# A hybrid attention block: the scores of a unit's two heads computed together, in three 64-row passes

## The chip, the cores and the metric

The kernel runs on one core of a Trainium2 chip. The metric is device time of one execution in microseconds, the median over several executions; lower is better. The times of the kernel before are 1458.97, 1459.27 and 1465.46 us, so its median is 1459.27 us.

## The reference, cut to what matters

One layer: a normalised input is projected, two kinds of attention run on it, and an output projection and a squared-ReLU MLP follow. The part that the change touches is the attention. There are 8 stick-breaking heads and 4 differential heads with two maps each, over 1024 positions; every head or map has 64 columns of q and of k:

```python
# stick-breaking, for each of 8 heads
z = jnp.einsum('bhqd,bhkd->bhqk', qb, kh) * scale          # d = 64
w = where(causal, exp(log_sigmoid(z) + reverse_cumsum(log_sigmoid(-z))), 0)
out = jnp.einsum('bhqk,bhkd->bhqd', w, vh)
# differential, for each of 4 heads, with two maps
s1 = einsum(q1, k1) * scale + bias;  s2 = einsum(q2, k2) * scale + bias   # d = 64
a = softmax(s1) - lam * softmax(s2)
out = jnp.einsum('bhqk,bhkd->bhqd', a, vh)
```

## The kernel before, in words

All matrix products are made from float32r parts: an operand is split into a high part and the rest (the low part), and a product is the sum of high x high, high x low and low x high.

The attention is worked in eight **units** (the loop at L511): units 0 to 3 hold two stick-breaking heads each (`steps_sb`, L312), units 4 to 7 hold one differential head with its two maps (`steps_diff`, L370). So a unit always has two score matrices, here called its two heads. Rows 0 to 63 of a projected q or k belong to the first, rows 64 to 127 to the second.

The score of one head uses all 128 rows of TensorE. `project_q` (L204) writes one tile `qs` for each head, with the high part of its q on its own 64 rows and the low part stacked on the other 64. `project_k` (L218) writes for each head a tile `kh` and a tile `kl`, whose own 64 rows are copied by four DMAs to the other 64 (L230, L231): the doubled k. `scores` (L259) then needs two passes for one head and one chunk of at most 512 keys: `qs` x `kh` (L262) and `qs` x `kl` (L263). Each chunk takes one bank of PSUM under the tag `sc`, of which there are two.

A head's queries are taken in blocks `qt` of 128, two blocks to a step `j`, steps in the order 3, 1, 2, 0; block `qt` has `(qt+1)*128` keys, so a block of more than 512 keys has two chunks. In a stick-breaking unit the first head's four steps come first, then the second's. ScalarE turns each chunk into `rest` and `beta` (two sigmoids, L322 and L323), GpSimd masks the diagonal (L326), VectorE scans and multiplies (L331, L332). In a differential unit VectorE adds the bias and finds the minimum (L389), ScalarE takes the exponential (L394). One step later `finish_sb` (L296) or `finish_diff` (L339) transposes the weights on TensorE (L281), splits them (L287, L288) and multiplies them by v into a bank with the tag `av` (two banks); `finish_diff` also takes a second `av` bank for a sum of squares.

Between the steps the generator `fill` (L480) gives TensorE other work: the projections of the next unit and the gate projections (L196 to L198). Each step has a weight, and `total` (L518) says how the filler is spread over them. The tile framework places all instructions on each engine's queue ahead of time; a queue runs in the order in which it was written. After the units come the mixing of the branches (L567), the output projection (L656), and the MLP (L778, L954).

Of the kernel before, what the change touches and what calls it, by code (L numbers as in the profile page):

```python
# [12 lines left out]
ALU = mybir.AluOpType  # L13
# [28 lines left out]
def hybrid_block_kernel(  # L42
# [24 lines left out]
    ps = ctx.enter_context(tc.tile_pool(name="ps", bufs=1, space=PSUM))  # L67
# [9 lines left out]
    def any_tile(name, tags=("acc", "sc", "av")):  # L77
        turn[0] += 1
        return ps.tile([P, HALF], F32, tag=tags[turn[0] % len(tags)], name=name, bufs=2)
# [70 lines left out]
    with ExitStack() as actx:  # L150
# [4 lines left out]
        def normalised(c):  # L155

            xs = []
            for t in range(4 * c, 4 * c + 4):
                if t == 6:
                    last = pa.tile([P, 2, D], F32, tag="v", name="x_67", bufs=3)  # L160
                if t < 6:
                    xt = pa.tile([P, D], F32, tag="big_s" if t < 4 else "kh", name=f"x_{t}", bufs=4)
# [40 lines left out]

        def project_q(blk, name, scale, qs):  # L204

            qs += [pa.tile([P, S], F32R, tag="qs", name=f"qs_{name}_{a}", bufs=4) for a in range(2)]

            def done(c, cs, acc):
                for a, (own, other) in enumerate(((LO, HI), (HI, LO))):
                    nc.scalar.activation(qs[a][own, cs], acc[own], AF.Copy, scale=scale)  # L210
# [7 lines left out]
        def project_k(blk, name, kh, kl):  # L218

            kh += [pa.tile([P, S], F32R, tag="kh", name=f"kh_{name}_{a}", bufs=4) for a in range(2)]  # L220
            kl += [pa.tile([P, S], F32R, tag="kl", name=f"kl_{name}_{a}", bufs=4) for a in range(2)]

            def done(c, cs, acc):
                for a, own in enumerate((LO, HI)):
                    nc.scalar.copy(kh[a][own, cs], acc[own])
                    nc.vector.tensor_tensor(kl[a][own, cs], acc[own], f32(kh[a][own, cs]), op=ALU.subtract)

            yield from project(blk, name, done)
            for a, (own, other) in enumerate(((LO, HI), (HI, LO))):
                nc.sync.dma_start(out=f32(kh[a][other]), in_=f32(kh[a][own]))  # L230
                nc.sync.dma_start(out=f32(kl[a][other]), in_=f32(kl[a][own]))  # L231

        def project_v(grp, name, diff, vs):

            parts = early.pop(name, None) or [load_split(w_v[2 * grp + i], f"{name}_{i}") for i in range(2)]
            vs += [pa.tile([P, NT, 2 * P], F32R, tag="v", name=f"v_{name}_{u}", bufs=3) for u in range(2)]
# [22 lines left out]
        def scores(qs, kh, kl, qt, c0, c1, name):  # L259
            z = ps.tile([P, HALF], F32, tag="sc", name=name, bufs=2)  # L260
            q = qs[:, qt * P:(qt + 1) * P]
            nc.tensor.matmul(z[:, :c1 - c0], q, kh[:, c0:c1], start=True, stop=False)  # L262
            nc.tensor.matmul(z[:, :c1 - c0], q, kl[:, c0:c1], start=False, stop=True)  # L263
            return z[:, :c1 - c0]

        def score_tile(qt, name):
            if qt < 4:
                return pa.tile([P, HALF], F32, tag="small_s", name=name, bufs=4)
            return pa.tile([P, S], F32, tag="big_s", name=name, bufs=4)

# [24 lines left out]

        def finish_sb(u, a, j, w, v):  # L296
            av = ps.tile([P, HALF], F32, tag="av", name=f"av_{u}_{a}_{j}", bufs=2)
            for kb, qc, hi, lo in transposed(w, j, f"sb{u}_{a}_{j}"):
# [3 lines left out]
            part = pa.tile([P, 256], F32, tag="part", name=f"part_{u}_{a}_{j}", bufs=4)[LO]  # L302
            nc.scalar.copy(part, av[HI, 0:256])
            nc.vector.tensor_tensor(part, av[LO, 0:256], part, op=ALU.add)
            yt = pa.tile([P, 2, 256], F32R, tag="yt", name=f"yt_{u}_{a}_{j}")
            nc.scalar.copy(yt[LO, 0, :], part)
            nc.vector.tensor_tensor(yt[LO, 1, :], part, f32(yt[LO, 0, :]), op=ALU.subtract)
            nc.sync.dma_start(
                out=y_dram[u][a * DH:(a + 1) * DH, :, j * 256:(j + 1) * 256], in_=f32(yt[LO])
            )  # L310

        def steps_sb(u, qs, kh, kl, v):  # L312
            for a in range(2):
                for j in ORDER:
                    w = []
                    for qt in (2 * j, 2 * j + 1):
                        nk = (qt + 1) * P
                        name = f"{u}_{a}_{qt}"
                        beta, rest = score_tile(qt, f"beta_{name}"), score_tile(qt, f"rest_{name}")
                        for c0, c1 in chunks(nk):  # L320
                            z = scores(qs[a], kh[a], kl[a], qt, c0, c1, f"z_{name}_{c0}")
                            nc.scalar.activation(rest[:, c0:c1], z, AF.Sigmoid, scale=-1.0)  # L322
                            last_sigmoid[0] = nc.scalar.activation(beta[:, c0:c1], z, AF.Sigmoid)  # L323
                        dg = slice(nk - P, nk)
                        for tl, fill in ((rest, 1.0), (beta, 0.0)):
# [4 lines left out]
                        back = rest[:, nk - 1::-1]  # L330
                        nc.vector.tensor_tensor_scan(back, back, back, 1.0, op0=ALU.mult, op1=ALU.bypass)  # L331
                        nc.vector.tensor_tensor(  # L332
                            beta[:, :nk - 1], beta[:, :nk - 1], rest[:, 1:nk], op=ALU.mult
                        )
                        w.append(beta)
                    yield 4 * j + 3, partial(finish_sb, u, a, j, w, v)


        def finish_diff(h, j, w, v):  # L339
            av = ps.tile([P, HALF], F32, tag="av", name=f"avd_{h}_{j}", bufs=2)[:, 0:256]  # L340
            for kb, qc, hi, lo in transposed(w, j, f"df{h}_{j}"):
# [3 lines left out]
            yt, sq, r, w = (  # L345
                pa.tile([P, 256], F32, tag="part", name=f"{n}_{h}_{j}", bufs=4) for n in ("y", "sq", "r", "w")
            )
            nc.scalar.copy(yt, av)

            nc.scalar.activation(sq, yt, AF.Square)  # L350
            both = pa.tile([P, 2, 256], F32R, tag="yt", name=f"sqp_{h}_{j}")
            nc.scalar.copy(both[:, 0, :], sq)
            nc.vector.tensor_tensor(both[:, 1, :], sq, f32(both[:, 0, :]), op=ALU.subtract)
            ss = ps.tile([P, HALF], F32, tag="av", name=f"ss_{h}_{j}", bufs=2)[:, 0:256]
# [10 lines left out]
            both = pa.tile([P, 2, 256], F32R, tag="yt", name=f"yp_{h}_{j}")  # L365
# [4 lines left out]
        def steps_diff(h, qs, kh, kl, v):  # L370
# [5 lines left out]
            for j in ORDER:  # L376
                w = []
                for qt in (2 * j, 2 * j + 1):
                    nk = (qt + 1) * P
                    probs = []  # L380
                    sums = pa.tile([P, 2], F32, tag="sums", name=f"sums_{h}_{qt}", bufs=4)
                    for m in range(2):
                        name = f"{h}_{m}_{qt}"
                        s = score_tile(qt, f"s_{name}")
                        low = None
                        for c0, c1 in chunks(nk):
                            z = scores(qs[m], kh[m], kl[m], qt, c0, c1, f"z_{name}_{c0}")
                            prev, low = low, pa.tile([P, 1], F32, tag="low", name=f"low_{name}_{c0}", bufs=6)
                            nc.vector.tensor_tensor_reduce(  # L389
                                out=s[:, c0:c1], in0=z, in1=bias[:, S - nk + c0:S - nk + c1],  # L390
                                scale=1.0, scalar=BIG if prev is None else prev,
                                op0=ALU.add, op1=ALU.min, accum_out=low,
                            )
                        e = nc.scalar.activation(  # L394
                            s[:, :nk], s[:, :nk], AF.Exp, bias=low, scale=-1.0,
                            accum_out=sums[:, m:m + 1],
                        )
                        after_sigmoids(e)
                        probs.append(s)
# [8 lines left out]
                yield 4 * j + 3, partial(finish_diff, h, j, w, v)  # L408
# [15 lines left out]
        def setup_bias():  # L424
# [3 lines left out]
            for c in range(3):  # L428
# [5 lines left out]
                bvec = pa.tile([N_DIFF, 384], F32, tag="yt", name=f"bvec_{c}")  # L434
# [28 lines left out]
        def prepare(u):  # L463
# [5 lines left out]
            qs, kh, kl = [], [], []  # L469
            yield from project_q(qblk + h, f"{name}q{h}", scale, qs)  # L470
            yield from project_k(kblk + h, f"{name}k{h}", kh, kl)
# [4 lines left out]
            operands[u] = (qs, kh, kl, vs[u])  # L476
# [15 lines left out]
        qs, kh, kl, pair = [], [], [], []  # L492
        parts = [project_q(SBQ, "sbq0", SCALE, qs), project_k(SBK, "sbk0", kh, kl), project_v(0, "sbv0", False, pair)]
        early["sbv0"] = [
            load_split(
                w_v[i], f"sbv0_{i}", *(pa.tile([P, S], F32R, tag=n, name=f"{n}_sbv0_{i}", bufs=4) for n in ("qs", "kl"))
            ) for i in range(2)
# [588 lines left out]
```

## Time and profile before

| what | value |
|---|---|
| median of the runs (lowest, highest) | 1459.27 us (1458.97, 1465.46) |
| span of the profiled execution | 1456.6 us |
| TensorE (PE) busy | 1435.0 us, 99% of the span |
| VectorE (DVE) busy | 1016.5 us |
| ScalarE (ACT) busy | 742.3 us |
| GpSimd (POOL) busy | 321.2 us |

The profile gives the span of its execution, 1456.6 us; the median of the timed runs is 2.7 us above that. PE is busy when a matmul is under way, and PEld is the loading of its stationary operand (its weights), which overlaps the matmul ahead of it. A matmul's listed duration has a tail in which the next one already streams, so what a matmul costs PE is the time from its start to the next one's start. In the rows, `out<-in` names what is written and read by the program's names; the last figures before `x` are partitions by elements.

### The profile page before, as it was taken

How to read it: one execution, taken by the hardware profiler on the slowest of the kernel's cores; microseconds unless marked ns; L12 is line 12 of the kernel's file. 1: busy time of each engine (PE TensorE's matmuls, PEld its weight loads, DVE VectorE, ACT ScalarE, POOL GpSimd, SP SyncE). 2: the span in 40 equal slices, each digit the busy share in tenths (PEclk: the TensorE clock that was granted, in tenths of full speed). 3: DMA queues.
4: the chain of work that ended last, by engine and by line, in shares of the span. 5: the costliest groups of instructions: out<-in, count | busy, mean ns of one | idle time of the engine just before them, and what ended most of it. 6: DMA issues, size and time to landing. Idle time of an engine off the chain costs nothing.

```text
span 1456.6 us, 20071 instructions
## 1 busy us (share of the span) xinstructions
PE 1435.0 (99%) x7302; PEld 1220.3 (84%) x7302; DVE 1016.5 (70%) x1468; ACT 742.3 (51%) x1352; POOL 321.2 (22%) x312
## 2 busy tenths in 40 slices
PE   7999999999999999999999999999999999999997
PEld 6888898899889888888888878888888888888886
DVE  5477988898779876635556499767665669754783
ACT  6355765676556554763335364444444443534350
POOL 2022322231000000000002335333330357232611
PEclk9999999999999999999999999999999999999999
DMA  5241212221322245553437745544446785677681
GB/s 206 73 138 64 72 48 81 65 73 48 83 85 66 75 122 180 162 196 139 162 120 244 238 151 195 187 151 142 143 161 205 252 286 178 209 243 273 197 287 58
DMA packets 93946, 220.50 MB, mean 151 GB/s; under 512 B 9260, under 2 KB 24856, under 8 KB 93848
## 3 DMA queue, kind: packets, MB, share of 16 engines
q1 hardware_dynamic: 79448, 199.30, 42.8%
q10 hardware_dynamic: 14400, 19.93, 3.8%
q8 instruction: 57, 0.93, 0.3%
q14 instruction: 41, 0.34, 0.1%
HBM read 153.11 MB, written 60.05 MB: 146 GB/s over the span
## 4 chain that ended last, share of the span: by engine, by line
PE 94%; DVE 2%; DMA 1%; issue 1%; ACT 1%; POOL 0%; SPq 0%; POOLq 0%; DVEq 0%; ACTq 0%
PE dS L954 12%; PE dA L954 9%; PE mix L567 6%; PE o L656 6%; PE p_tr L778 5%; PE p_av L778 5%; PE c L778 4%; PE acc_gate L198 4%; PE acc_gate L196 4%; PE acc_gate L197 4%; PE p_sc L778 3%; PE z L263 2%; PE z L262 2%; PE tr_sb L281 2%; PE p L778 1%
## 5 line engine op out<-in xcount | busy, mean ns | idle before, releaser
L331 DVE TENSOR_TENSOR_SCAN rest<-rest 128x896 f32<-128x896 f32 (+3 forms) x64 | 87.6, 1374 | 20.6 <-POOL rest L326 20.3
L198 PE MATMUL acc_gate<-h_hi,lo_gate 128*128 128x512 f32 x256 | 101.0, 394 | 0.0
L196 PE MATMUL acc_gate<-h_hi,hi_gate 128*128 128x512 f32 x256 | 100.8, 394 | 0.0
L197 PE MATMUL acc_gate<-h_lo,hi_gate 128*128 128x512 f32 x256 | 100.7, 394 | 0.0
L608 DVE TENSOR_TENSOR lS_lo<-raw_S,lS_hi 128x1024 fp32r<-128x1024 f32 x32 | 56.2, 1757 | 39.8 <-ACT lS_hi L607 39.8
L326 POOL TENSOR_SCALAR_AFFINE_SELECT rest<-rest 128x128 f32<-128x128 f32 x64 | 23.5, 367 | 240.7 <-ACT rest L322 232.1
L954 PE MATMUL dS<-rT_hi,lS_hi 128*128 128x512 f32 x192 | 74.7, 389 | 0.0
L954 PE MATMUL dS<-rT_lo,lS_hi 128*128 128x512 f32 x192 | 74.7, 389 | 0.0
L954 PE MATMUL dS<-rT_hi,lS_lo 128*128 128x512 f32 x192 | 74.7, 389 | 0.0
L607 ACT CAST lS_hi<-raw_S 128x1024 fp32r<-128x1024 f32 x32 | 33.7, 1052 | 74.1 <-DMA raw_S<-s_dramS 33.8
L567 PE MATMUL mix<-y,hi_mix 128*128 128x512 f32 x256 | 68.6, 389 | 0.0
L394 ACT ACTIVATE s<-s,low 128x896 f32<-128x896 f32 (+7 forms) x64 | 49.7, 777 | 29.9 <-DVE low L389 29.7
L389 DVE CUSTOM_DVE_ANT_0 s<-z,bias 128x512 f32<-128x512 f32 (+3 forms) x64 | 37.0, 587 | 32.4 <-PE z L263 26.4
L567 PEld LDWEIGHTS mix<-y,hi_mix 128*128 128x128 f32 x256 | 48.0, 188 | 10.0
L198 PEld LDWEIGHTS acc_gate<-h_hi,lo_gate 128*128 128x128 f32 x256 | 48.2, 188 | 9.2
L197 PEld LDWEIGHTS acc_gate<-h_lo,hi_gate 128*128 128x128 f32 x256 | 48.2, 188 | 8.8
L196 PEld LDWEIGHTS acc_gate<-h_hi,hi_gate 128*128 128x128 f32 x256 | 48.2, 188 | 8.6
L116 POOL TENSOR_SCALAR rstd_o<-s 128x1 f32<-128x1 f32 x8 | 2.8, 356 | 236.5 <-DVE wa_lo L608 212.2
L287 ACT CAST wth_sb<-tr_sb 128x512 fp32r<-128x512 f32 (+1 forms) x80 | 41.2, 548 | 26.6 <-PE tr_sb L281 25.2
L326 POOL TENSOR_SCALAR_AFFINE_SELECT beta<-beta 128x128 f32<-128x128 f32 x64 | 53.9, 842 | 3.4 <-ACT beta L323 2.4
L288 DVE TENSOR_TENSOR wtl_sb<-tr_sb,wth_sb 128x512 fp32r<-128x512 f32 (+1 forms) x80 | 48.5, 627 | 7.7 <-ACT wth_sb L287 7.5
L778 PE MATMUL c<-hB_hi,wa_hi 128*128 128x512 f32 x128 | 50.0, 392 | 2.1 <-ACT p L798 2.1
(351 smaller groups left out, 4751.2 us busy)
## 6 DMA issues: line engine op xcount, KB each, us to landing
s_dramS<-us SPq DMA_DIRECT2D x64, 256.0 KB, 3.9
raw_S<-s_dramS SPq DMA_DIRECT2D x32, 512.0 KB, 4.4
s_dramA<-u ACTq DMA_DIRECT2D x48, 256.0 KB, 3.5
raw_A<-s_dramA SPq DMA_DIRECT2D x24, 512.0 KB, 3.8
raw_gate<-in_w_in_dram SPq DMA_DIRECT2D x16, 512.0 KB, 3.7
gate_dram<-gt SPq DMA_DIRECT2D x32, 256.0 KB, 2.5
y<-y_dram SPq DMA_DIRECT2D x16, 512.0 KB, 6.4
g<-gate_dram SPq DMA_DIRECT2D x16, 512.0 KB, 4.3
```

The costliest lines, as they stand in the source:

```text
L196: nc.tensor.matmul(acc, w_hi[:, ks], h_hi[k][:, cs], start=(k == 0), stop=False)
L197: nc.tensor.matmul(acc, w_hi[:, ks], h_lo[k][:, cs], start=False, stop=False)
L198: nc.tensor.matmul(acc, w_lo[:, ks], h_hi[k][:, cs], start=False, stop=(k == NK - 1))
L288: nc.vector.tensor_tensor(lo[:, :n], tr[:, :n], f32(hi[:, :n]), op=ALU.subtract)
L326: nc.gpsimd.affine_select(tl[:, dg], tl[:, dg], pattern=[[-1, P]], compare_op=ALU.is_gt, fill=fill, base=0, channel_multiplier=1,)
L331: nc.vector.tensor_tensor_scan(back, back, back, 1.0, op0=ALU.mult, op1=ALU.bypass)
L394: e = nc.scalar.activation(s[:, :nk], s[:, :nk], AF.Exp, bias=low, scale=-1.0, accum_out=sums[:, m:m + 1],)
L567: nc.tensor.matmul(accs[i][c], st[:, ks], mv[:, cs], start=(first and k % 4 == 0), stop=(last and k % 4 == 3),)
L608: nc.vector.tensor_tensor(lo, raw, f32(hi), op=ALU.subtract)
L656: nc.tensor.matmul(accs[n], st, mv[:, n * HALF:(n + 1) * HALF], start=(first and k == 0), stop=(last and k == NK - 1),)
L778: nc.tensor.matmul(acc, st[:, ks], mv, start=(first and k == 0 and i == 0), stop=(k == 3 and i == 2), skip_group_check=True,)
L954: nc.tensor.matmul(acc, st[:, e, ts], mv[:, e, :], start=(first and e == 0 and i == 0), stop=(last and e == 1 and i == 2))
```

## The change

The high and low parts of q are now two plain tiles `qh` and `ql`, and those of k `kh` and `kl`, each with both heads on their halves of the rows. Nothing is stacked, nothing doubled, and the four DMAs of a unit's k are gone. `scores` makes both heads of a chunk in one call: three passes (high x high, high x low, low x high), and in each pass one matmul on rows 0 to 63 for the first head and one on rows 64 to 127 for the second, into two banks. A step of a stick-breaking unit now works both heads side by side, so the unit has four steps of two blocks instead of eight; a step is left once in its middle for filler (`yield 4 * j + 1, None`), and its two finishes follow in the next two places.

PSUM is dealt out anew: three `sc` banks instead of two, one `av` bank instead of two. `finish_sb` puts both heads into halves of one bank and evicts them together; `finish_diff` keeps its product and its sum of squares in halves of one bank. The pool of banks is closed after the units and opened again.

```diff
-    ps = ctx.enter_context(tc.tile_pool(name="ps", bufs=1, space=PSUM))
+    BANKS_OF = {"acc": 2, "tr": 2, "sc": 3, "av": 1}
+    pctx = ExitStack()
+    ps = pctx.enter_context(tc.tile_pool(name="ps", bufs=1, space=PSUM))
...
+            qs += [operand(tag, name) for tag in ("qh", "ql")]
+            hi, lo = qs
             def done(c, cs, acc):
-                for a, (own, other) in enumerate(((LO, HI), (HI, LO))):
-                    nc.scalar.activation(qs[a][own, cs], acc[own], AF.Copy, scale=scale)
-                    nc.vector.scalar_tensor_tensor(
-                        qs[a][other, cs], acc[own], scale, f32(qs[a][own, cs]),
-                        op0=ALU.mult, op1=ALU.subtract,
-                    )
+                nc.scalar.activation(hi[:, cs], acc, AF.Copy, scale=scale)
+                nc.vector.scalar_tensor_tensor(lo[:, cs], acc, scale, f32(hi[:, cs]), op0=ALU.mult, op1=ALU.subtract)
...
             yield from project(blk, name, done)
-            for a, (own, other) in enumerate(((LO, HI), (HI, LO))):
-                nc.sync.dma_start(out=f32(kh[a][other]), in_=f32(kh[a][own]))
-                nc.sync.dma_start(out=f32(kl[a][other]), in_=f32(kl[a][own]))
...
-        def scores(qs, kh, kl, qt, c0, c1, name):
-            z = ps.tile([P, HALF], F32, tag="sc", name=name, bufs=2)
-            q = qs[:, qt * P:(qt + 1) * P]
-            nc.tensor.matmul(z[:, :c1 - c0], q, kh[:, c0:c1], start=True, stop=False)
-            nc.tensor.matmul(z[:, :c1 - c0], q, kl[:, c0:c1], start=False, stop=True)
-            return z[:, :c1 - c0]
+        def scores(qs, ks, qt, c0, c1, name):
+            zs = [ps.tile([P, HALF], F32, tag="sc", name=f"{name}_{a}", bufs=3)[:, :c1 - c0] for a in range(2)]
+            passes = ((qs[0], ks[0]), (qs[0], ks[1]), (qs[1], ks[0]))
+            for i, (st, mv) in enumerate(passes):
+                for a, rows in enumerate((LO, HI)):
+                    nc.tensor.matmul(
+                        zs[a], st[rows, qt * P:(qt + 1) * P], mv[rows, c0:c1], start=(i == 0), stop=(i == 2)
+                    )
+            return zs
...
+            if a == 0:
+                both_av[u, j] = ps.tile([P, 2, 256], F32, tag="av", name=f"av_{u}_{j}", bufs=1)
+            av = both_av[u, j][:, a, :]
...
-            av = ps.tile([P, HALF], F32, tag="av", name=f"avd_{h}_{j}", bufs=2)[:, 0:256]
+            bank_of_j = ps.tile([P, 2, 256], F32, tag="av", name=f"avd_{h}_{j}", bufs=1)
+            av, ss = bank_of_j[:, 0, :], bank_of_j[:, 1, :]
...
+                    if qt == 2 * j:
+                        yield 4 * j + 1, None
+                yield 4 * j + 5, [partial(finish_sb, u, a, j, w[a], v) for a in range(2)]
...
-            total = 36 * (2 if u < N_SB else 1)
+            total = 48
```

How the three passes come to stand in TensorE's queue is seen in the order of the program. The first place is the start of unit 1, whose first block is 6 (896 keys, chunks of 512 and 384). In the kernel before, PE has there (in `z_1_0_6_512`: unit 1, head 0, block 6, the chunk that starts at key 512):

```order
L281 MATMUL tr_sb0_1_2_1_1542<-ident_69,beta_0_1_5_1423 128x128
L262 MATMUL z_1_0_6_0_1576<-kh_sbk1_0_955,qs_sbq1_0_804 128x512
L263 MATMUL z_1_0_6_0_1576<-kl_sbk1_0_957,qs_sbq1_0_804 128x512
L262 MATMUL z_1_0_6_512_1581<-kh_sbk1_0_955,qs_sbq1_0_804 128x384
L263 MATMUL z_1_0_6_512_1581<-kl_sbk1_0_957,qs_sbq1_0_804 128x384
L198 MATMUL acc_sbq2_1_1667<-h_hi3_158,lo_sbq2_1635 128x512
```

With the change PE has at that place (in `z_1_6_512_0`: unit 1, block 6, the chunk from key 512, head 0, the head last):

```order
L264 MATMUL z_1_6_0_0_1533<-kh_sbk1_856,qh_sbq1_794 128x512
L264 MATMUL z_1_6_0_1_1534<-kh_sbk1_856,qh_sbq1_794 128x512
L264 MATMUL z_1_6_0_0_1533<-kl_sbk1_857,qh_sbq1_794 128x512
L264 MATMUL z_1_6_0_1_1534<-kl_sbk1_857,qh_sbq1_794 128x512
L264 MATMUL z_1_6_0_0_1533<-kh_sbk1_856,ql_sbq1_795 128x512
L264 MATMUL z_1_6_0_1_1534<-kh_sbk1_856,ql_sbq1_795 128x512
L200 MATMUL acc_sbq2_1_1617<-h_lo7_170,hi_sbq2_1586 128x512
L201 MATMUL acc_sbq2_1_1617<-h_hi7_162,lo_sbq2_1587 128x512
L264 MATMUL z_1_6_512_0_1545<-kh_sbk1_856,qh_sbq1_794 128x384
L264 MATMUL z_1_6_512_0_1545<-kl_sbk1_857,qh_sbq1_794 128x384
L264 MATMUL z_1_6_512_0_1545<-kh_sbk1_856,ql_sbq1_795 128x384
L199 MATMUL acc_sbk2_0_1652<-h_hi0_155,hi_sbk2_1648 128x512
```

The first chunk stands there as it was written, the heads in turn. Of the second chunk only the first head's three passes follow, with a projection on 128 rows ahead of them and behind them. The second place is where the second head's three passes come and block 7 begins, some fifty rows further on:

```order
L201 MATMUL acc_sbk2_1_1739<-h_hi2_157,lo_sbk2_1649 128x512
L264 MATMUL z_1_6_512_1_1546<-kh_sbk1_856,qh_sbq1_794 128x384
L264 MATMUL z_1_6_512_1_1546<-kl_sbk1_857,qh_sbq1_794 128x384
L264 MATMUL z_1_6_512_1_1546<-kh_sbk1_856,ql_sbq1_795 128x384
L264 MATMUL z_1_7_0_0_1683<-kh_sbk1_856,qh_sbq1_794 128x512
L310 MATMUL av_0_2_1416<-wth_sb0_0_2_2_1447,v_sbv0_0_383 128x256
L264 MATMUL z_1_7_0_0_1683<-kl_sbk1_857,qh_sbq1_794 128x512
L264 MATMUL z_1_7_0_1_1684<-kh_sbk1_856,qh_sbq1_794 128x512
L264 MATMUL z_1_7_0_1_1684<-kl_sbk1_857,qh_sbq1_794 128x512
L264 MATMUL z_1_7_0_0_1683<-kh_sbk1_856,ql_sbq1_795 128x512
L264 MATMUL z_1_7_0_1_1684<-kh_sbk1_856,ql_sbq1_795 128x512
L199 MATMUL acc_sbk2_1_1739<-h_hi3_158,hi_sbk2_1648 128x512
```

Here the heads' passes stand partly in turn and partly one behind the other, and a product with v on 128 rows stands between two of them.

More of the change, by code (lines that the diff above doesn't have):

```diff
@@ L216, in project_q, with project_k @@
             yield from project(blk, name, done)
-        def project_k(blk, name, kh, kl):
-            kh += [pa.tile([P, S], F32R, tag="kh", name=f"kh_{name}_{a}", bufs=4) for a in range(2)]
-            kl += [pa.tile([P, S], F32R, tag="kl", name=f"kl_{name}_{a}", bufs=4) for a in range(2)]
+        def project_k(blk, name, ks):
+            ks += [operand(tag, name) for tag in ("kh", "kl")]
+            hi, lo = ks
             def done(c, cs, acc):
-                for a, own in enumerate((LO, HI)):
-                    nc.scalar.copy(kh[a][own, cs], acc[own])
-                    nc.vector.tensor_tensor(kl[a][own, cs], acc[own], f32(kh[a][own, cs]), op=ALU.subtract)
+                nc.scalar.copy(hi[:, cs], acc)
+                nc.vector.tensor_tensor(lo[:, cs], acc, f32(hi[:, cs]), op=ALU.subtract)
@@ L269, in score_tile, with other_tile @@
             return pa.tile([P, S], F32, tag="big_s", name=name, bufs=4)
+        def other_tile(qt, name):
+            return pa.tile([P, S], F32, tag="rest", name=name, bufs=2)[:, :(qt + 1) * P]
         def chunks(n):
@@ L308, in finish_sb @@
[L308 to L325, printed above, removed]
+            if a == 0:
+                return
@@ new lines, in finish_sb @@
+            av = both_av.pop((u, j))
+            part = pa.tile([P, 2, 256], F32, tag="part", name=f"part_{u}_{j}", bufs=2)[LO]
+            nc.scalar.copy(part, av[HI])
+            nc.vector.tensor_tensor(part, av[LO], part, op=ALU.add)
+            yt = pa.tile([P, 2, 2, 256], F32R, tag="yt", name=f"yt_{u}_{j}", bufs=1)[LO]
+            nc.scalar.copy(yt[:, 0], part)
+            nc.vector.tensor_tensor(yt[:, 1], part, f32(yt[:, 0]), op=ALU.subtract)
+            for e in range(2):
+                nc.sync.dma_start(
+                    out=y_dram[u][e * DH:(e + 1) * DH, :, j * 256:(j + 1) * 256], in_=f32(yt[:, :, e, :])
+                )
@@ new lines, in steps_sb @@
+        def steps_sb(u, qs, ks, v):
+            for j in ORDER:
+                w = [[], []]
+                for qt in (2 * j, 2 * j + 1):
+                    nk = (qt + 1) * P
+                    names = [f"{u}_{a}_{qt}" for a in range(2)]
+                    rest = [other_tile(qt, f"rest_{n}") for n in names]
+                    beta = [weight_tile(qt, f"beta_{n}") for n in names]
+                    for c0, c1 in chunks(nk):
+                        zs = scores(qs, ks, qt, c0, c1, f"z_{u}_{qt}_{c0}")
+                        for a in range(2):
+                            nc.scalar.activation(rest[a][:, c0:c1], zs[a], AF.Sigmoid, scale=-1.0)
+                            last_sigmoid[0] = nc.scalar.activation(beta[a][:, c0:c1], zs[a], AF.Sigmoid)
+                    dg = slice(nk - P, nk)
+                    for a in range(2):
+                        for tl, fill in ((rest[a], 1.0), (beta[a], 0.0)):
@@ L364, in finish_diff @@
             nc.vector.scalar_tensor_tensor(yt, yt, subln, w, op0=ALU.mult, op1=ALU.mult)
-            both = pa.tile([P, 2, 256], F32R, tag="yt", name=f"yp_{h}_{j}")
+            both = pages[:, 1]
             nc.scalar.copy(both[:, 0, :], yt)
@@ L506, in hybrid_block_kernel @@
                 pass
-        operands[0] = (qs, kh, kl, pair[0])
+        operands[0] = (qs, ks, pair[0])
         vs[1] = pair[1]
         setup_bias()
-        waiting = None
+        waiting = []
         for u in range(n_units):
@@ L528, in hybrid_block_kernel @@
                 pass
-        waiting()
+        for finish in waiting:
+            finish()
         for b in range(GATES[-1].stop, 2 * NK):
```

108 lines of the change are left out of this document (51 added, 57 removed).

## The prediction

> **What bounds the kernel now.** The first things to read are the page's span, its busy times and the chain that ended last.
>
> ```profile
> span 1456.6 us, 20071 instructions
> PE 1435.0 (99%) x7302; PEld 1220.3 (84%) x7302; DVE 1016.5 (70%) x1468; ACT 742.3 (51%) x1352; POOL 321.2 (22%) x312
> PE 94%; DVE 2%; DMA 1%; issue 1%; ACT 1%; POOL 0%; SPq 0%; POOLq 0%; DVEq 0%; ACTq 0%
> ```
>
> PE is busy for 99% of the span and holds 94% of the chain. The next view is the busy time by stretches, cut at the start of the units (64 us), at the first differential unit (346) and at the end of the last (645); its columns are us, then PE, PEld, DVE, ACT and POOL busy with their instruction counts, PE's granted clock, DMA share and GB/s.
>
> ```profile
> 64.00:346.00 282.00, 280.41 (x1729) 248.94 (x1728) 238.74 (x340) 179.28 (x413) 75.74 (x129) 1.00 0.26 73
> 346.00:645.00 299.00, 299.00 (x1669) 260.46 (x1668) 213.98 (x548) 176.93 (x373) 0.43 (x3) 1.00 0.37 117
> ```
>
> The two attention stages that the change touches last 282 and 299 us, and PE idles 1.6 us in both together (282.00 - 280.41, then nothing). So a microsecond that PE's queue gains or loses there is one in the total, until another engine is late; DVE, with 238.74 of 282, is nearest to that.
>
> Busy time does not price a matmul. What counts is the time from one start to the next, read from PE's timeline (start, duration, instruction):
>
> ```profile
> 701.25 1.07 PE L567 MATMUL mix<-y,hi_mix 128*128 128x512 f32 x4
> 702.16 0.61 PE L567 MATMUL mix<-y,lo_mix 128*128 128x512 f32 x2
> 702.61 0.39 PE L567 MATMUL mix<-y,hi_mix 128*128 128x512 f32 x1
> 63.98 0.28 PE L244 MATMUL acc_sbv<-kl_sbv,h_hi 128*128 128x256 f32 x1
> 64.10 0.28 PE L245 MATMUL acc_sbv<-qs_sbv,h_lo 128*128 128x256 f32 x1
> ...
> 87.27 0.22 PE L262 MATMUL z<-kh_sbk,qs_sbq 128*128 128x128 f32 x1
> 87.33 0.28 PE L263 MATMUL z<-kl_sbk,qs_sbq 128*128 128x128 f32 x1
> 87.44 0.34 PE L300 MATMUL av<-wth_sb,v_sbv 128*128 128x256 f32 x1
> ```
>
> Six matmuls of 512 columns take 702.61 - 701.25 = 1.36 us, 0.227 each; 256 columns take 0.12; 128 columns take 0.06 where the next one has the same weights (L262 and L263 share `qs`) and 0.11 where it has others, because new weights need 0.11. For 384 columns, rows further down give 65.79 - 65.62 = 0.17.
>
> **The streams of the scores.** The view of the tile `z` gives the matmuls of the stick-breaking units; the differential units have the same numbers.
>
> ```profile
> L262 PE MATMUL z<-kh_sbk,qs_sbq x96: 220/389/500, 65.0 to 343.2; 128*128 128x512 f32 x48, 128*128 128x384 f32 x16, 128*128 128x128 f32 x16, 128*128 128x256 f32 x16
> L263 PE MATMUL z<-kl_sbk,qs_sbq x96: 272/368/478, 65.4 to 343.4; 128*128 128x512 f32 x48, 128*128 128x384 f32 x16, 128*128 128x128 f32 x16, 128*128 128x256 f32 x16
> ```
>
> Before, that is 4 x 48 = 192 of 512 columns and 64 each of 384, 256 and 128: 192 x 0.227 + 64 x 0.17 + 64 x 0.12 + 32 x (0.06 + 0.11) = 43.6 + 10.9 + 7.7 + 5.4 = **67.6 us**.
>
> After, three passes for each head make 576 matmuls on 64 rows. Two of them can share a stream only where they use different halves of the rows and stand next to each other in PE's queue. In the order of the changed program 133 such pairs stand (98 whose longer one has 512 columns, 19 of 384, 10 of 256, 6 of 128), and 310 matmuls have no partner (105, 52, 74 and 79): there are three banks, a chunk wants two, and the second head's passes often come dozens of rows later. A pair that overlaps costs one stream, but not less than two loads of weights, 0.22: 98 x 0.227 + 35 x 0.22 = 29.9. The singles cost 105 x 0.227 + 52 x 0.17 + 74 x 0.12 + 79 x 0.09 = 48.7 (0.09 is the mean of 0.06, 0.11 and 0.11). The sum is 78.6 us: **11 us more** than before, although the pairs overlap. No row shows two matmuls on different halves of the rows, so the pair is bounded: one stream (0.227) or two (0.454). With two streams, 288 x 0.227 + 96 x (0.17 + 0.12 + 0.09) = 101.9, or 34 more. I take one stream: the two share no row and no bank, and the rows above show that the array starts a matmul as soon as the stream ahead is in, without waiting for its 0.39 us to end.
>
> The Trainium skill (TensorE: Matmul & The Clock Gate, Part 3: Packing small matmuls) has matmuls in distinct row groups run together, four of 32 rows at 3.07 times the speed of one after the other. By that share a pair would cost about 1.3 streams at worst, some 7 us on top of the 11; no run here shows it yet.
>
> **The switch between 128 and 64 rows.** The 576 matmuls stand in 147 stretches, 62 of them of just three matmuls, between others on 128 rows. That makes 294 changes of the shape in which the array is used; before there are four, around the small product of the bias setup (L433, 32 rows). The first two of these price a change (PE's timeline, then rows of PEld's and of ScalarE's):
>
> ```profile
> 64.31 0.80 PE L433 MATMUL bp<-oh,tbl 32*4 32x384 f32 x2
> 65.05 0.50 PE L262 MATMUL z<-kh_sbk,qs_sbq 128*128 128x512 f32 x1
> 65.38 0.40 PE L263 MATMUL z<-kl_sbk,qs_sbq 128*128 128x512 f32 x1
> 65.62 0.33 PE L262 MATMUL z<-kh_sbk,qs_sbq 128*128 128x384 f32 x1
> 65.79 0.34 PE L263 MATMUL z<-kl_sbk,qs_sbq 128*128 128x384 f32 x1
> ...
> 63.99 0.19 PEld L245 LDWEIGHTS acc_sbv<-qs_sbv,h_lo 128*128 128x128 f32 x1
> 65.05 0.19 PEld L262 LDWEIGHTS z<-kh_sbk,qs_sbq 128*128 128x128 f32 x1 [0.65 <-ACT v_sbv L254]
> ...
> 64.42 0.27 ACT L254 CAST v_sbv<-acc_sbv 128x128 fp32r<-128x128 f32 x1 [1.99 <-PE acc_sbv L245]
> ```
>
> Into 32 rows: the matmul at 64.10 should be followed 0.12 later, at 64.22; the next starts at 64.31, 0.09 late. Back to 128 rows: two streams of 0.32 from 64.31 end at 64.95; the weights of `z` load at 65.05, 0.09 to 0.10 late. The profile names ScalarE's cast as releaser, but that cast ended at 64.42 + 0.27 = 64.69. And within a shape the next weights load while a matmul streams (63.99, just after the matmul of 63.98 began), so they cost nothing; here they load only afterwards, and the first `z` takes 65.38 - 65.05 = 0.33 instead of 0.23. A change therefore costs 0.09 + 0.11 = 0.20 us when 128 columns of weights follow, as they do everywhere here. It is cheaper only where the first instruction of a stretch waits for ScalarE or VectorE anyway, which in these stages is 1.6 us in all. 290 more changes x 0.20 = **58 us**. Nothing hides it, since it is PE's own time. The lower bound is nothing, if 64 rows differ from the 32 of these rows.
>
> The Trainium skill (TensorEngine Tiling (Array Packing), Key Properties) says that changing the tiling mode, not just the tile, drains TensorE, 64-row modes included; that speaks against this change and makes the lower bound less likely, but no row here is of 64 rows.
>
> **What is costed at nothing.** Two halves of q or k are evicted by one instruction instead of two, and the copies of k fall away:
>
> ```profile
> L230 SPq DMA_DIRECT2D kh_sbk<-kh_sbk x8: 491/540/837, 55.3 to 244.1; - x8
> L210 ACT ACTIVATE qs_sbq<-acc_sbq x16: 583/592/594, 31.1 to 226.7; 64x512 fp32r<-64x512 f32 x16
> ...
> PE z L262 <- ACT beta L323: 0.3, 1, 0.3
> ...
> L303 ACT COPY part<-av x32: 367/369/371, 96.6 to 363.5; 64x256 f32<-64x256 f32 x32
> L304 DVE TENSOR_TENSOR part<-av,part x32: 389/408/418, 97.6 to 364.0; 64x256 f32<-64x256 f32 x32
> ```
>
> That frees ScalarE of 16 x 0.59 us in a stage where it is busy for 179 of 282, and SP's queue of its part; PE's list of waits has 0.3 us for `z` and no DMA of k in it. The single `av` bank makes a step's product wait until the last one's eviction is done. A step lies about 299 / 16 = 19 us of PE work ahead of the next, far more than the eviction; uncovered, the copy and the addition (0.37 + 0.41) would cost 0.78 us in each of 32 steps, 25 us, and I leave this to the range. The same holds for the third `sc` bank.
>
> **The sum.** Against the profiled execution: 1456.6 + 11 + 58 = 1525.6 us of span. The median of the runs is 2.7 above that span: **1528 us**.
>
> **The rivals.**
> - *The pairs do not overlap*: 34 in place of 11, 1459 + 34 + 58 = 1551. For it: no row shows two halves at once. Chance 0.15.
> - *In 64-row use the weights of the same half are not loaded ahead*: 98 times a single follows on the same half with other weights, 0.11 each, 11 us more: 1539. The Trainium skill (TensorE: Matmul & The Clock Gate, What overlaps and what doesn't) says that weights load beside a matmul only when the row group differs. The rows at 63.98 and 63.99 speak against it, since both use all rows. Chance 0.12.
> - *The switch to 64 rows is nearly free*: 11 us of streams, and up to 20 us of waits for banks and DVE that the switches would have covered (an estimate, a third of their 58 us): 1470 to 1490. Chance 0.20.
> - *Faster*: the array runs the other half's matmuls ahead wherever a half is free, and switches cost nothing. All 288 pairs then take half of the 101.9 us, 51, which is 17 less than before: 1442. It turns at 17 / 290 = 0.06 us for a switch; the trace has 0.20, and the order puts only 133 pairs side by side. This is also the case in which the change does what its words say, two heads together everywhere. Chance 0.05.
>
> **How the numbers follow.** The forecast has 0.48. The range, 1482 to 1558, takes in both dear rivals and the upper end of the cheap switch, and leaves out the rest of that rival and the faster one. A measurement of this kernel tells 0.5%, 7 us, from no change. Faster by more than that: 0.05, the last rival; within it: 0.05, the part of the cheap switch that has hardly any waits; slower: 0.90, the rest.
>
> **What would show it.** In the profile after, `z` has 576 matmuls; a pair's starts lie some ns apart if it overlaps, 0.227 us if not. At each change of rows the weights load about 0.09 us after the stream ahead is in, and the first matmul's start-to-start is 0.11 longer. PE stays at 98 to 99% in both stages, the stages grow by about 69 us together, and everything after them keeps its length. The prediction is wrong if weights load ahead across such a change, or if waits of PE for ACT or DVE take the place of the switches.

## The result, and the profile after

| | before | after |
|---|---|---|
| median of four runs each (lowest, highest) | 1459.86 us (1458.97, 1465.46) | 1531.98 us (1530.08, 1535.23) |
| ratio, 95% interval | 1 | 1.0489 (1.0463 to 1.0515): slower |
| profiled execution | span 1456.6 us | own time 1535.23 us, span 1533.4 us |

The profile after is of the execution that took longest (granted clock 0.991 of the span; 0.992, 0.995 and 0.995 in the others), 3 us above the median; its span lies 1.8 us below its own time. The page's span, busy times and chain after the change:

```profile
span 1533.4 us, 20225 instructions
PE 1504.9 (98%) x7494; PEld 1228.5 (80%) x7494; DVE 992.4 (65%) x1405; ACT 720.4 (47%) x1287; POOL 318.0 (21%) x312
PE 92%; DMA 3%; DVE 2%; ACT 1%; issue 1%; SPq 0%; POOL 0%; ACTq 0%; DVEq 0%; POOLq 0%
```

DVE lost 24 us of work, ACT 22, and neither shows in the time: PE was and is what ends last. The view by stretches, cut at 64, 370 and 710 us (the first score starts at 59.1, the first differential one at 384.4), in the same columns as before:

```profile
64.00:370.00 306.00, 304.94 (x1757) 245.67 (x1757) 213.64 (x278) 157.93 (x345) 71.28 (x117) 0.98 0.18 52
370.00:710.00 340.00, 339.16 (x1840) 269.09 (x1840) 216.60 (x550) 177.07 (x377) 6.03 (x15) 1.00 0.29 95
```

PE idles 1.06 us in the first and 0.84 in the second. The growth is therefore PE's own. PE's list of waits (what it waited for; us in all, times, longest) has nothing that could be the 72 us. Its first line, at the start of the kernel, is there before as well (7.7 us); the wait for `gt` lies behind the last unit:

```profile
PE trx L181 <- DVE x L173: 8.4, 3, 7.3
PE mix L587 <- ACT gt L473: 3.1, 1, 3.1
PE c L798 <- ACT p L818: 2.8, 1, 2.8
...
PE z L264 <- ACT beta L338: 1.1, 1, 1.1
```

Next the start of unit 1, the first place that the order of the program showed. PE's timeline (start, duration, instruction) and then that of the weight loads:

```profile
153.82 1.06 PE L287 MATMUL tr_sb<-ident,beta 128*128 128x128 f32 x8
154.81 0.50 PE L264 MATMUL z<-kh_sbk,qh_sbq 64*128 64x512 f32 x2
155.15 0.40 PE L264 MATMUL z<-kl_sbk,qh_sbq 64*128 64x512 f32 x2
155.38 0.39 PE L264 MATMUL z<-kh_sbk,ql_sbq 64*128 64x512 f32 x2
155.70 0.50 PE L200 MATMUL acc_sbq<-h_lo,hi_sbq 128*128 128x512 f32 x1
156.04 0.40 PE L201 MATMUL acc_sbq<-h_hi,lo_sbq 128*128 128x512 f32 x1
156.37 0.44 PE L264 MATMUL z<-kh_sbk,qh_sbq 64*128 64x384 f32 x1
```

```profile
154.81 0.19 PEld L264 LDWEIGHTS z<-kh_sbk,qh_sbq 64*128 64x128 f32 x2 [0.17 <-ACT part L316]
154.92 0.19 PEld L264 LDWEIGHTS z<-kl_sbk,qh_sbq 64*128 64x128 f32 x2
155.15 0.19 PEld L264 LDWEIGHTS z<-kh_sbk,ql_sbq 64*128 64x128 f32 x2
155.70 0.19 PEld L200 LDWEIGHTS acc_sbq<-h_lo,hi_sbq 128*128 128x128 f32 x1 [0.36 <-issue]
155.81 0.19 PEld L201 LDWEIGHTS acc_sbq<-h_hi,lo_sbq 128*128 128x128 f32 x1
```

Three things are to be seen. **A pair is one stream**: the second pair runs from 155.15 to 155.38, 0.23 us for two matmuls of 512 columns (the trace's records put the two starts of a pair 1 to 15 ns apart, nearly all of them 3 to 10). **A change of rows waits**: the third pair's stream is in at 155.38 + 0.23 = 155.61, and the next matmul, on 128 rows, starts at 155.70, 0.09 later. **And its weights lie open**: L200's weights load at 155.70, with its matmul, not ahead of it, so that its start-to-start is 156.04 - 155.70 = 0.34 instead of 0.227; the first pair likewise takes 155.15 - 154.81 = 0.34. Inside the stretch the weights of the next pass load 0.11 after the first pair's start, while it streams. These few rows hold two whole changes for one stream saved (three where the kernel before has four).

The sum over all such rows: for each of PE's matmuls up to the first of the mixing stage I take the time to the next start and subtract its own stream (0.227, 0.17, 0.114 or 0.057 us by its columns; a pair counts once).

| up to the first `mix`, us | before | after | more |
|---|---|---|---|
| first matmul to the first `mix` | 640.7 | 714.6 | +73.9 |
| streams of the scores | 65.4 | 72.8 (132 pairs 27.3, the rest 45.5) | +7.4 |
| excess at a change of rows: ahead of it 36.0, in the first matmul behind it 26.3 | 0.4 | 62.3 | +61.9 |
| excess under a halved clock | 0 | 5.3 | +5.3 |
| 24 gate matmuls that stand behind the first `mix` in the kernel before | 0 | 5.4 | +5.4 |

These four add up to 80.0. The rest is -6.1, mostly excess between scores that is not at a change (7.6 before, 0.5 after). The gate matmuls are only moved, so the units themselves grew by 73.9 - 5.4 = 68.5 us. What comes after, the mixing stage included, takes 811.5 us (1533.4 - 721.9) where it took 808.4 (1456.6 - 648.2), although those 5.4 us are gone from it: 8.5 us more. PE's clock is halved there from 721.9 to 727.6, from 864.2 to 867.6 and from 932.4 to 935.9, with PE busy throughout, which is 6.3 of the 8.5.

### The profile page after: what moved, and what is told of

It reads as the page before. It is cut to its first block, busy times and chain, and to the rows that moved or that the text cites. A ratio compares the mean times of both kernels' runs of the same rounds, so it can differ in the third digit from the quotient of the medians.

```text
span 1533.4 us, 20225 instructions
## 1 busy us (share of the span) xinstructions
PE 1504.9 (98%) x7494; PEld 1228.5 (80%) x7494; DVE 992.4 (65%) x1405; ACT 720.4 (47%) x1287; POOL 318.0 (21%) x312
## 4 chain that ended last, share of the span: by engine, by line
PE 92%; DMA 3%; DVE 2%; ACT 1%; issue 1%; SPq 0%; POOL 0%; ACTq 0%; DVEq 0%; POOLq 0%
PE dS L974 11%; PE dA L974 9%; PE z L264 7%; PE mix L587 6%; PE p_tr L798 5%; PE p_av L798 5%; PE c L798 5%; PE acc_gate L199 4%; PE acc_gate L200 4%; PE acc_gate L201 4%; PE p_sc L798 3%; PE o L676 2%; PE tr_sb L287 2%; PE av L311 1%; PE av L310 1%; PE p L798 1%
## 5 line engine op out<-in xcount | busy, mean ns | idle before, releaser
L347 DVE TENSOR_TENSOR_SCAN rest<-rest 128x896 f32<-128x896 f32 (+7 forms) x64 | 87.8, 1373 | 25.6 <-POOL rest L342 25.1
L200 PE MATMUL acc_gate<-h_lo,hi_gate 128*128 128x512 f32 x256 | 101.2, 395 | 0.0
L342 POOL TENSOR_SCALAR_AFFINE_SELECT rest<-rest 128x128 f32<-128x128 f32 x64 | 32.9, 514 | 268.2 <-ACT rest L337 247.7
L337 ACT ACTIVATE rest<-z 128x512 f32<-128x512 f32 (+3 forms) x96 | 47.8, 500 | 51.9 <-DVE beta L348 42.9
L199 PEld LDWEIGHTS acc_gate<-h_hi,hi_gate 128*128 128x128 f32 x256 | 48.1, 188 | 11.4 <-issue 2.0
L200 PEld LDWEIGHTS acc_gate<-h_lo,hi_gate 128*128 128x128 f32 x256 | 48.1, 188 | 10.7 <-issue 1.3
L201 PEld LDWEIGHTS acc_gate<-h_hi,lo_gate 128*128 128x128 f32 x256 | 48.1, 188 | 10.2 <-issue 0.7
L348 DVE TENSOR_TENSOR beta<-beta,rest 128x895 f32<-128x895 f32 (+7 forms) x64 | 48.4, 762 | 4.5 <-POOL beta L342 1.4
L798 PE MATMUL c<-hB_lo,wa_hi 128*128 128x512 f32 x128 | 50.5, 395 | 0.0
```

Source lines behind the costliest of these rows:

```text
L199: nc.tensor.matmul(acc, w_hi[:, ks], h_hi[k][:, cs], start=(k == 0), stop=False)
L200: nc.tensor.matmul(acc, w_hi[:, ks], h_lo[k][:, cs], start=False, stop=False)
L201: nc.tensor.matmul(acc, w_lo[:, ks], h_hi[k][:, cs], start=False, stop=(k == NK - 1))
L348: nc.vector.tensor_tensor(beta[a][:, :nk - 1], beta[a][:, :nk - 1], rest[a][:, 1:nk], op=ALU.mult)
L798: nc.tensor.matmul(acc, st[:, ks], mv, start=(first and k == 0 and i == 0), stop=(k == 3 and i == 2), skip_group_check=True,)
```

## The experiments

Theory S: a change between 128 and 64 rows costs about 0.2 us of PE, and the 294 changes are the loss. Rival L: the two heads worked side by side, with the new deal of banks, cost the time by waits. Rival T: the pairs do not really share. The first five runs measure the price by itself, in the mixing stage of the kernel before, where 64 more matmuls write a bank that nobody reads; the next five take the changed kernel apart.

### The price of a change alone

The control adds 64 matmuls on all rows, `d64` the same 64 on rows 0 to 63 (128 more changes), `d64pair` 64 pairs on both halves.

```diff
+            spare = [ps.tile([P, HALF], F32, tag="tr", name=f"spare{b}_{e}", bufs=2) for e in range(2)]
             for k in range(NK):
...
+                # d128
+                nc.tensor.matmul(spare[0], w_hi[:, ks], y_hi[:, :HALF], start=True, stop=True)
+                # d64
+                nc.tensor.matmul(spare[0], w_hi[LO, ks], y_hi[LO, :HALF], start=True, stop=True)
+                # d64pair
+                for e, rows in enumerate((LO, HI)):
+                    nc.tensor.matmul(spare[e], w_hi[rows, ks], y_hi[rows, :HALF], start=True, stop=True)
```

Expected of `d128`: 

> The kernel before with one more matmul on all 128 rows, 512 columns, for each of the 8 x 8 steps of the mixing stage, into a spare bank that nobody reads. It is the control for the next two. Both theories: 64 x 0.227 = 14.5 us more than before, about 1474 us.

Measured: 1477.48 us, 1.0117 (1.0098 to 1.0136), 16.6 above the kernel before as measured beside it (1460.9), where 64 streams are 14.5.

Expected of `d64`: 

> The same 64 extra matmuls, but on rows 0 to 63 only; the rest of the kernel before stays. 128 more changes between 128 and 64 rows. If a change costs 0.09 us of waiting and 0.11 us of exposed weights: 14.5 + 128 x 0.20 = 40 us more than before, about 1500 us. If changes are free, and the loss of the changed kernel comes from its order and its banks: the same as the control, about 1474 us.

Measured: 1501.09 us, 1.0280 (1.0264 to 1.0295). The same work on half the rows costs 23.6 us more, **0.184 us for each of 128 changes**. The two timelines of PE, first of `d128`, then of `d64`:

```profile
659.84 0.39 PE L565 MATMUL spare<-y,hi_mix 128*128 128x512 f32 x1
660.07 1.07 PE L569 MATMUL mix<-y,hi_mix 128*128 128x512 f32 x4
660.97 0.62 PE L569 MATMUL mix<-y,lo_mix 128*128 128x512 f32 x2
```

```profile
660.10 0.50 PE L565 MATMUL spare<-y,hi_mix 64*128 64x512 f32 x1
660.52 1.18 PE L569 MATMUL mix<-y,hi_mix 128*128 128x512 f32 x4
661.54 0.61 PE L569 MATMUL mix<-y,lo_mix 128*128 128x512 f32 x2
```

On all rows the next start is 0.23 us behind the spare one, on half of them 0.42 = 0.227 + 0.11 + 0.09, and the four behind it take 1.02 instead of 0.90 (the weights of the first lie open again). No bank, loop or engine differs, so the changes alone do this.

Expected of `d64pair`: 

> As the last, but each extra matmul on rows 0 to 63 has a partner on rows 64 to 127 right behind it, into a second spare bank: 128 extra matmuls in 51 stretches. If a pair takes one stream and a change costs 0.20 us: 64 x 0.227 + 102 x 0.20 = 35 us more than before, about 1495 us. If a pair takes two streams: 14 us more than that, about 1509 us.

Measured: 1497.08 us, 1.0245 (1.0223 to 1.0266). The scheduler merged some stretches, so there are 102 changes, not 128: 26 fewer at 0.184 make 1496.3. The 64 additional matmuls on the other half cost 0.8 us together, less than the spread of the runs (1494.59 to 1498.75), where 64 streams are 14.5. Rival T falls for matmuls that stand side by side.

The next two gather the 64 pairs into 8 groups of 8 (20 more changes), in `d64group` with the halves in turn, in `d64apart` with the eight lower ones queued ahead of the eight upper ones (so it stands in seven of the groups; in both kernels the scheduler broke up the first):

```diff
+            for k in range(NK):
+                for e, rows in enumerate((LO, HI)):
+                    nc.tensor.matmul(
+                        spare[e], w_hi[rows, k * P:(k + 1) * P], y[k][0][rows, :HALF], start=True, stop=True
+                    )
...
-            for k in range(NK):
-                for e, rows in enumerate((LO, HI)):
+            for e, rows in enumerate((LO, HI)):
+                for k in range(NK):
```

Expected of `d64group`: 

> The kernel before with the 64 extra pairs on 64 rows, as in the run with pairs, but the eight pairs of a block of the mixing stage stand together: 20 more changes of rows instead of 102. If the change of rows is the price and not the pair: 64 x 0.227 + 20 x 0.20 = 19 us more than before, about 1479 us. If matmuls on 64 rows are dear in themselves: as with single pairs, 1497 us.

Measured: 1481.02 us, 1.0140 (1.0124 to 1.0156), 3.5 above `d128`: 20 changes at 0.184 are 3.7. Twice as many matmuls, on half the rows each, run in the time of 64 on all rows once the changes are few.

Expected of `d64apart`: 

> The kernel before with the 64 extra pairs in groups of eight as in the run in groups, but in the queue the eight matmuls on rows 0 to 63 stand ahead of the eight on rows 64 to 127. If TensorE starts a half's matmuls ahead of earlier ones of the other half: the same as that run, 1479 to 1483 us. If it keeps the order of the queue: hardly a stream is shared, about 55 of 64, some 13 us more, about 1494 us.

Measured: 1488.08 us, 1.0208 (1.0190 to 1.0226), between the two. One group in PE's timeline, `d64group` first; the second fence is `d64apart`, shown in three pieces, and each piece but the first counts one matmul that began in the piece ahead of it:

```profile
669.08 2.12 PE L564 MATMUL spare<-y,hi_mix 64*128 64x512 f32 x16
671.12 1.19 PE L573 MATMUL mix<-y,hi_mix 128*128 128x512 f32 x4
```

```profile
668.28 1.20 PE L564 MATMUL spare<-y,hi_mix 64*128 64x512 f32 x4
...
669.09 1.44 PE L564 MATMUL spare<-y,hi_mix 64*128 64x512 f32 x9
...
670.13 1.31 PE L564 MATMUL spare<-y,hi_mix 64*128 64x512 f32 x5
```

In turn, 16 matmuls take 2.04 us (671.12 - 669.08), eight streams and their change. Apart, four begin alone in the first microsecond, eight in the next, four alone in the last, and the group takes 3.09 (671.37 - 668.28). Since two of the same half do not share (in `e6_same_half`, below, no two scores start within 40 ns of each other), this reads as: TensorE starts matmuls of the free half ahead of earlier ones of the busy half, but reaches only about four ahead. By the traces the seven whole groups take 1.04 us more each and the broken one 0.59, 7.9 us in all; the medians differ by 7.1. Neither of the two expectations had a limited reach.

### The changed kernel taken apart

In `e1_heads_apart` the two loops of `scores` are exchanged, so that the queue holds three passes of one head and then three of the other, as far as the scheduler leaves them:

```diff
-            for i, (st, mv) in enumerate(passes):
-                for a, rows in enumerate((LO, HI)):
+            for a, rows in enumerate((LO, HI)):
+                for i, (st, mv) in enumerate(passes):
```

Expected: 

> The changed kernel with the two loops of the scores exchanged: the three passes of the first head, then those of the second. In the program's order 78 pairs stand side by side instead of 133, and there are 286 changes of rows instead of 294. If a pair that stands side by side saves a stream: streams of 90 us instead of 79, 11 us more, less 8 x 0.2, so about 1541 us. If the side by side does not matter: 1530 us.

Measured: 1534.42 us, 1.0506 (1.0484 to 1.0529): no difference from the changed kernel that can be told, although its queue has 78 pairs side by side instead of 133. In PE's timeline the place shown above reads the same:

```profile
155.33 0.51 PE L264 MATMUL z<-kh_sbk,qh_sbq 64*128 64x512 f32 x2
155.67 0.40 PE L264 MATMUL z<-kl_sbk,qh_sbq 64*128 64x512 f32 x2
155.91 0.40 PE L264 MATMUL z<-kh_sbk,ql_sbq 64*128 64x512 f32 x2
156.23 0.50 PE L200 MATMUL acc_sbq<-h_lo,hi_sbq 128*128 128x512 f32 x1
```

Pass 1 of both heads runs together, then pass 2, then pass 3, though the queue has the first head's three passes ahead of the second's. In all, 128 pairs start within 40 ns of each other. The expectation that only neighbours share fell; three ahead is within the reach that `d64apart` showed.

`e2_all_rows` keeps the loops, banks and three passes, but every score matmul uses all rows: none of the changes, and no sharing. `e6_same_half` keeps the changes but puts both heads on rows 0 to 63: no sharing.

```diff
-                for a, rows in enumerate((LO, HI)):
+                for a in range(2):                          # e2_all_rows
...
-                        zs[a], st[rows, qt * P:(qt + 1) * P], mv[rows, c0:c1], start=(i == 0), stop=(i == 2)
+                        zs[a], st[:, qt * P:(qt + 1) * P], mv[:, c0:c1], start=(i == 0), stop=(i == 2)
...
-                for a, rows in enumerate((LO, HI)):
+                for a, rows in enumerate((LO, LO)):         # e6_same_half
```

Expected of `e2_all_rows`: 

> The changed kernel with every score matmul on all 128 rows instead of 64 (so each head's score is the sum of both heads' here): the same 576 matmuls, loops, banks and filler, but no change of rows and no pair. If the 294 changes of rows are the loss: streams of 102 us, 34 more than before, and no changes, so 1494 us, plus waits that the changes had covered, up to 1505. If the loss comes from the loops and banks: 23 us more than the changed kernel, 1555 us.

Measured: 1507.77 us, 1.0324 (1.0307 to 1.0341), a little above the band of S and far below 1555.

Expected of `e6_same_half`: 

> The changed kernel with both heads' score matmuls on rows 0 to 63 (so the second head's score repeats the first's): the same instructions, order, stretches and changes of rows, but no two matmuls can share a stream. If sharing saves what the sum says: streams of 102 us instead of 79, 23 us more than the changed kernel, about 1555 us. If sharing saves nothing on the path: 1532 us.

Measured: 1559.60 us, 1.0680 (1.0662 to 1.0698).

With these two, the way from before to after is a chain of measured steps. A third pass on all rows, with its loops: 1507.77 - 1459.86 = 47.9 us, of which half as many streams again as before are 65.4 / 2 = 32.7. The same 576 unshared streams (98.1 us), on 64 rows and with 294 changes: 1559.60 - 1507.77 = **51.8 us, 0.176 for each**. Sharing between the halves: 1531.98 - 1559.60 = **-27.6 us**, of which the streams are 72.8 - 98.1 = -25.3. The third pass and the changes cost 99.7 us, 3.6 times what the sharing saves.

`e6_same_half` also settles whether weights of the same half load ahead. Its timeline has three passes of one head in a row:

```profile
160.31 0.44 PE L264 MATMUL z<-kh_sbk,qh_sbq 64*128 64x384 f32 x1
160.59 0.34 PE L264 MATMUL z<-kl_sbk,qh_sbq 64*128 64x384 f32 x1
160.77 0.33 PE L264 MATMUL z<-kh_sbk,ql_sbq 64*128 64x384 f32 x1
161.04 0.50 PE L199 MATMUL acc_sbk<-h_hi,hi_sbk 128*128 128x512 f32 x1
```

After the open load of the first (0.28) the next start comes 0.18 later, a bare stream of 384 columns, and the third pass, which has other weights on the same half, takes 161.04 - 160.77 = 0.27: its stream and the wait at the change behind it, with no open load.

The last two ask what the rest of the change costs when no change of rows covers it. `e3_all_rows_two` has all rows and two passes, so the streams of before with the loops and banks of after; `e7_old_banks` is that with the old deal of banks.

```diff
-            passes = ((qs[0], ks[0]), (qs[0], ks[1]), (qs[1], ks[0]))
+            passes = ((qs[0], ks[0]), (qs[0], ks[1]))       # e3_all_rows_two, with the rows of e2_all_rows and stop=(i == 1)
...
-    BANKS_OF = {"acc": 2, "tr": 2, "sc": 3, "av": 1}
+    BANKS_OF = {"acc": 2, "tr": 2, "sc": 2, "av": 2}        # e7_old_banks, with the bufs of the score and av tiles to match
```

Expected of `e3_all_rows_two`: 

> As the last, and the third pass (low part of q by high part of k) is left out: 384 score matmuls on 128 rows, the same streams as before, in the loops and banks of the change. If all but the 64 rows costs nothing, as the prediction has it: 1460 us. If the new loops and banks bring waits of their own that the changes of rows cover: up to 1495 us. If they and not the rows are the loss: 1520 us.

Measured: 1493.12 us, 1.0216 (1.0193 to 1.0238): the dear end. The streams are those of before, so some 33 us come from the loops, the banks and the buffers. Two of its waits of PE, and then the view from the first score to the first `mix`, of `e3_all_rows_two`, of `e2_all_rows` and of the changed kernel:

```profile
PE avd L375 <- ACT yp L373: 9.0, 2, 7.0
...
PE z L264 <- ACT beta L338: 5.5, 6, 1.5
```

```profile
59.20:680.20 621.00, 600.36 (x3481) 523.62 (x3479) 432.94 (x836) 337.15 (x732) 78.56 (x132) 0.99 0.26 82
59.10:694.10 635.00, 629.35 (x3672) 552.61 (x3670) 434.60 (x837) 339.64 (x733) 80.01 (x132) 1.00 0.25 79
59.10:721.90 662.80, 657.80 (x3672) 526.25 (x3671) 434.88 (x836) 341.11 (x734) 77.31 (x132) 0.99 0.24 76
```

PE idles 20.6 us in `e3_all_rows_two`, 5.7 in `e2_all_rows` and 5.0 in the changed kernel. One place is the score that waits for a bank until ScalarE is done with it (5.5 us). The longest single wait, 7.0 us, is for no bank. It is the sum of squares (L375) of the last step, behind the last filler matmul of the units (666.5):

```profile
675.78 0.53 SPq L388 DMA_DIRECT2D y_dram<-yp  x1
678.29 0.40 ACT L373 CAST yp<-ysq 128x256 fp32r<-128x256 f32 x1 [2.28 <-DMA y_dram<-yp]
678.75 0.58 PE L375 MATMUL avd<-yp,ones 128*128 128x256 f32 x1 [7.01 <-ACT yp L373]
```

ScalarE's cast waits until the DMA has read the tile `yp` of the step before. The change keeps the squares and the finished product in one tile `yp` with a single buffer, where the kernel before has a tile for each, in two buffers.

So rival L is real as a cost, but it is covered in the changed kernel. The changes of rows are not needed for that: `e2_all_rows` has none of them, and with the third pass alone PE idles hardly more than in the changed kernel. Its 32.7 us of streams more than `e3_all_rows_two` cost only 1507.77 - 1493.12 = 14.7 us. The PE work that the change adds makes PE late to those places. This is why costs do not add: by the table above the streams and the changes are 69 us, and yet the changed kernel is only 1531.98 - 1493.12 = 38.9 above `e3_all_rows_two`. Of the 30 us between, 15.6 are seen as PE's idle time that goes away and 6.9 as excess between scores (7.4 to 0.5); the rest I did not place.

Expected of `e7_old_banks`: 

> The kernel with all rows and two passes, but with the banks dealt as before the change: two for scores and two for the products with v, instead of three and one. If the single bank for the products is what costs 33 us there: back towards 1460 to 1475 us. If two heads side by side are short of banks for scores: slower than the 1493 us, about 1520 us.

Measured: 1524.91 us, 1.0445 (1.0424 to 1.0465). Giving the bank back to `av` costs 32 us more, so in these loops the third score bank is worth more than a second one for the product; both together would be nine banks, where the two kernels deal out eight. How the 32 us come about is not shown: up to 11 of them are a lower granted clock (0.983 of 1521.8 us against 0.990 of 1492.6), PE's listed waits for a score bank grow only from 5.5 us to 8.0, and the wait at L375 is there as well, 11.4 us.

## Why the prediction held

Predicted 1528 us, 1482 to 1558; measured 1531.98. By its own steps:

- *What bounds the kernel.* Held. PE idles 1.9 us in the two stretches of the units, and 24 us less of DVE and 22 less of ACT are worth nothing there.
- *The streams of the scores, +11.* The sign and the sharing were right, the term a little high: +7.4. It charged short singles and short pairs with open weights; the first matmuls of a stretch carry them, and they were in the price of a change as well. The pair as one stream, chosen between 0.227 and 0.454, is seen in the rows at 155.15 and 155.38 and in `d64pair`, where the second half costs 0.8 us for 64 matmuls. The 1.3 streams worked out from the Trainium skill (TensorE: Matmul & The Clock Gate, Part 3: Packing small matmuls) for a pair are more than what was measured here.
- *"Two of them can share a stream only where they ... stand next to each other in PE's queue".* This sentence was wrong, though it did no harm to the sum. `e1_heads_apart` has 78 neighbours and 128 shared streams; `d64apart` shows a reach of about four. The 133 counted pairs and the 132 of the trace agree because in this order the partners that are not neighbours are mostly dozens of rows away, which is luck as far as the sentence goes. The Trainium skill (TensorE: Matmul & The Clock Gate, Part 3, What overlaps and what doesn't) has matmuls start strictly in program order; on two halves of the rows the measurement differs.
- *The switch, 0.20 us, 290 times, +58.* Right, and in its two parts: 0.09 of waiting and 0.11 of open weights stand in the rows at 155.38 to 156.04. Measured 0.184 alone (`d64` less `d128`), 0.176 net in the changed kernel (`e6_same_half` less `e2_all_rows`), 0.21 gross in its trace (62.3 / 294). The four changes of before, to 32 rows, were a good model for 64. That weights load only after a change agrees with the drain of the Trainium skill (TensorEngine Tiling (Array Packing), Key Properties).
- *Costed at nothing.* True of the changed kernel (PE's wait for `z` is 1.1 us in all) and wrong as a reason. The prediction named PE work between the steps as the cover, and kept 25 us of uncovered `av` for the range. `e3_all_rows_two` shows that this cover is not enough: with the streams of before, the loops, banks and buffers cost about 33 us. What covers them is the PE time that the change adds, and `e2_all_rows` shows that the third pass alone does most of it. The longest wait there is for the single buffer of `yp`, which the prediction did not name.
- *The sum.* The units grew by 68.5 us where it has 69, and this is in part luck: the streams are 4 us below their term and the changes 4 above theirs, and 5.3 us under a halved clock are made up by the excess between scores that went away. That everything behind the units keeps its length did not hold: 8.5 us more, of which 6.3 are halved clock.
- *The rivals.* "The pairs do not overlap", 1551, has its twin in `e6_same_half`, 1559.6; the trace refutes it. Weights of the same half do load ahead (rows at 160.59 and 160.77). The nearly free switch, 1470 to 1490, is about what would be left without the changes (1531.98 - 51.8 = 1480, an estimate, since costs do not add here), but a change costs 0.18. The faster rival turned at 0.06 us for a change; half of its mechanism is true (the other half is run ahead, within a reach of four), the other half, free changes, is not.

## What to carry to other kernels

Count how often TensorE's queue goes from full rows to half rows and back before splitting a contraction: here a change costs 0.18 to 0.21 us, nearly one stream of 512 columns (0.227), and a stretch has two. Three shared passes of 64 rows instead of two times two of 128 save one stream in four for each chunk; with all 288 pairs shared that is 65.4 - 98.1 / 2 = 16 us here (98.1 are the unshared streams of `e6_same_half`), which about 90 changes eat up, so stretches would have to hold a dozen matmuls or more, and each needs its score banks at the same time; that was not tried. And a wait that seems to cost nothing may be hidden by work that the same change adds: undo the two apart, as `e3_all_rows_two` does, before counting on what is left.

## What the hardware showed beside that

Matmuls on different halves of the rows start out of the order of the queue, up to about four ahead (`d64apart`: four alone, eight shared, four alone). The section on the kernel before says that a queue runs in the order in which it was written; for such matmuls that is not so.

The clock was halved for stretches inside the changed kernel, where the kernel before shows none until 1452 us. Two of the four, by stretches (the number behind POOL's is the granted clock):

```profile
64.00:68.90 4.90, 3.85 (x24) 2.69 (x24) 1.01 (x3) 3.04 (x6) 0.00 (x0) 1.00 0.00 1
68.90:79.10 10.20, 10.20 (x22) 4.93 (x21) 7.22 (x7) 4.22 (x11) 6.66 (x4) 0.50 0.04 17
...
714.00:720.80 6.80, 4.79 (x22) 3.64 (x21) 1.98 (x3) 3.08 (x4) 0.00 (x0) 1.00 0.10 40
720.80:727.60 6.80, 5.71 (x13) 4.51 (x14) 2.28 (x6) 3.13 (x6) 0.00 (x0) 0.50 0.35 117
```

Each time PE idles there: 1.05 us (4.90 - 3.85) just ahead of the first, and in the 3.1 us wait for `gt` at the second (2.0 of them ahead of it, 6.80 - 4.79). The first lasts 10.2 us, with PE busy throughout, the second 6.8. So a wait of 1 us was followed by a loss of some 5 us more. Other waits had no such sequel: in the kernel before PE waits 2.1 us at once at L778, and its clock stays whole. What decides it was not tested.
